# Compressed branch's product on 128 rows, gates kept as 1 / gate, negated scale behind the rope

## The chip, the cores and the metric

The kernel runs on one core of one Trainium2 chip. Times are device microseconds (us) of that core; the time of a kernel is the median of its runs. The engines are TensorE (PE; its weight loads are listed as PEld), VectorE (DVE), ScalarE (ACT), GpSimd (POOL) and SyncE (SP, which issues most DMAs).

## What is computed

A decoder trunk of four layers over 256 tokens of 1024 features. Each layer is a token mixer and a squared-ReLU MLP, both with an RMS norm ahead and a residual sum. The change lies in the first layer's mixer, an attention with three branches per head: keys and values compressed over blocks of 32 tokens at stride 16 (15 blocks), selected blocks (here with 256 tokens all blocks that are not in the future), and a window. Each branch has its own softmax, and a sigmoid gate per token and head weighs its output. Cut to that:

```python
def _nsa_mixer(h, w_in, q_gain, k_gain, cmp_pos, w_cmp, w_out, cos, sin):
    q, kc, vc, ks, vs, kw, vw, gates = jnp.split(h @ w_in, ...)
    q = _apply_rope(_rms_norm(q, q_gain), cos, sin)          # 8 heads of 128
    kc, ks, kw = [_apply_rope(_rms_norm(k, k_gain[i]), cos, sin) for i, k in ...]
    gates = jax.nn.sigmoid(gates)
    kc = jnp.einsum('bnlgd,lde->bnge', kc[:, cidx] + cmp_pos[0], w_cmp[0])
    vc = jnp.einsum('bnlgd,lde->bnge', vc[:, cidx] + cmp_pos[1], w_cmp[1])
    ...
    p_c = _masked_softmax(q kc * scale, cmp_end <= t)
    o_c = jnp.einsum('bqghn,bngd->bqghd', p_c, vc)
    ... # p_s, o_s of the selected blocks; p_w, o_w of the window
    o = g[:, :, 0] * o_c + g[:, :, 1] * o_s + g[:, :, 2] * o_w
    return o @ w_out
```

## The kernel before

Everything is float32, and products with weights are made of three float32r products: each weight is split into a rounded part wh (ACT, L159) and the rest wl (DVE, L160), and L184 to L186 multiply them with the two parts of the input. Tokens lie in two tiles t of 128.

The function `nsa` projects in six chunks (`chunk`, 384 or 512 columns; 280 with the gates), into queries, keys and values. Chunks 0 to 3 give all keys, the first group's values, the gates and the queries of heads 0 to 3; `compress` makes the compressed keys (in `kcat`) and values `vcmp`, 32 rows of which two groups of 15 are used. Then come attention passes (`attend`) over units of a head h and a token tile t. The first pass has the eight units of heads 0 to 3; chunks 4 and 5 bring the second group's values and the queries of heads 4 to 7; the second pass has the eight units of these. The output products (`Out`, L212 to L214, "acc" in the trace) follow.

For a unit, `scores` adds masks and products of queries and keys in PSUM (t = 0: L579 to L583, t = 1: L594 to L604), takes maxima (DVE, L585, L606, L609), multiplies them with `nrq`, the negated scale of the query (L611), and ACT makes the exponentials of the three branches with their sums (L615). From the sums DVE makes the branches' weights in three steps, L618 (a maximum with 1e-30), L619 (the reciprocal) and L620 (times the gate), and scales the exponentials with them (L622, L623). `mix` then transposes the scaled exponentials on PE (L633 for two branches, L637 for the 32 compressed columns), ACT copies them to SBUF (PT, L635, and PTc, L639), and PE adds up the three branches in one accumulator `po`: two or four products with 128 rows (L642) and, last, one with 32 rows (L643). Each of these products is two instructions in the trace. ACT and DVE split the result (L89, L90).

`queries` computes the scale `rq` of each query with a power on POOL (in `head_scale`, L385), then `nrq` on DVE (L471), then the rope on DVE (L392, L393, L402), and queues the transposes (L459).

The order of the instructions on each engine is set by the scheduler of the layer under the kernel; it takes them from the order in which the code stands and from what it reckons to be ready. Each engine runs its own queue in order. In the passes the scheduler puts projection products (L184 to L186) and output products between the units' work on PE. Here the gates' lines before:

```python
gt = wp.tile([P, 24], F32, tag="gt", name="gt")
nc.scalar.activation(gt, o[:, 256:280], AF.Exp, scale=nrx[t])
nc.vector.tensor_scalar(gt, gt, 1.0, None, op0=ALU.add)
nc.vector.reciprocal(gates[:, t].rearrange("p a b -> p (a b)"), gt)
```

Of the kernel before, what the change touches and what calls it, by code (L numbers as in the profile page):

```python
# [10 lines left out]
F32 = mybir.dt.float32  # L11
F32R = mybir.dt.float32r
AF = mybir.ActivationFunctionType
ALU = mybir.AluOpType
AX = mybir.AxisListType

P = 128
# [6 lines left out]
DH = 128  # L24
# [43 lines left out]
def trunk(ctx: ExitStack, tc: tile.TileContext, A: dict, out: bass.AP):  # L68
    nc = tc.nc
# [354 lines left out]
    def nsa(n, first):  # L424
        aT = n.xT
        nxt = start_norm(4)
        with tc.tile_pool(name="nsa", bufs=1) as sp:
# [9 lines left out]
            gates = sp.tile([P, NT, NH, 3], F32, name="gates")  # L437
            rq = sp.tile([P, NT, NH], F32, name="rq")
            nrq = sp.tile([P, NT, NH], F32, name="nrq")
            vcmp = sp.tile([32, DH], F32, name="vcmp")  # L440
            quarters = sp.tile([P, 32], F32, name="quarters")
            oT = act.tile([P, KT, 2, NT, P], F32R, tag="aT", name="oT")
            with tc.tile_pool(name="nsw", bufs=2) as wp:
# [24 lines left out]
                def queries(t, src, h0, nh):  # L468
                    v = src.rearrange("p (h d) -> p h d", d=DH)
                    head_scale(wp, v, nh, he[t], rq[:, t, h0:h0 + nh])  # L470
                    nc.vector.tensor_scalar(nrq[:, t, h0:h0 + nh], rq[:, t, h0:h0 + nh], -1.0, None, op0=ALU.mult)  # L471
                    r = rope(wp, src, nh, G[:, t, 0, 0:1].to_broadcast([P, nh, DH]),
                             G[:, t, 1, 0:1].to_broadcast([P, nh, DH]))
                    transpose_to([(qT[:, h0:h0 + nh, t * P:(t + 1) * P], (0, nh))], [r[:, h] for h in range(nh)])


# [7 lines left out]
                def chunk(ci):  # L484
                    width = (offs[ci + 1] - offs[ci]) // 8
                    if ci == 0:
                        views = col_chunk(A["nsa_w"], 0, width, first)
                        ahead.extend(col_chunk(A["nsa_w"], offs[1], width, None, (0,)))
                        gain_tables(nc.vector, G, A["rope"], A["nsa_gain"], A["nsa_gsw"], 4)
                    elif ci == 1:  # L490
                        views = ahead + col_chunk(A["nsa_w"], offs[1], width, None, (1,))
                    else:
                        views = col_chunk(A["nsa_w"], offs[ci], width)
                    os_ = proj(aT, views, width, "AC")
                    for t in range(NT):
                        o = os_[t]
                        ts_ = slice(t * P, (t + 1) * P)
                        if not he:
                            stats()
                        if ci == 0:  # L500
                            kn = normed(wp, o[:, :256], 2, he[t])
                            r = rope(wp, kn, 2, G[:, t, 0, 1:2].to_broadcast([P, 2, DH]),
                                     G[:, t, 1, 1:2].to_broadcast([P, 2, DH]))
                            vc = wp.tile([P, 2, DH], F32, tag="vc", name="vc")
                            nc.scalar.mul(vc, o[:, 256:].rearrange("p (a b) -> p a b", b=P), rx[t])
                            cols = [kcT[:, kv, :, 1 + 16 * t:17 + 16 * t].rearrange("p r (n g) -> p g n r", g=2)
                                    for kv in range(2)]
                            transpose_to([(cols[0], (0, 2)), (cols[1], (2, 4))],
                                         [r[:, 0], r[:, 1], vc[:, 0], vc[:, 1]])
                        elif ci == 1:  # L510
                            kn = normed(wp, o, 4, he[t])
                            g1, g2 = ([G[:, t, i, 2 + k:3 + k].to_broadcast([P, 2, DH]) for k in range(2)]
                                      for i in range(2))
                            r = rope(wp, kn, 4, g1, g2, True)
                            base = 288 * t
                            transpose_to([(kcat[:, :, base:base + P], (0, 2)),
                                          (kcat[:, :, base + P:base + 2 * P], (2, 4))], [r[:, h] for h in range(4)])
                        elif ci == 2:
                            queries(t, o, 0, 4)
                        elif ci == 5:  # L520
                            queries(t, o[:, :384], 5, 3)
                        else:
                            g = ci - 3
                            nc.scalar.mul(vv[:, t, :, g], o[:, :256].rearrange("p (a b) -> p a b", b=P), rx[t])
                            if ci == 3:
                                gt = wp.tile([P, 24], F32, tag="gt", name="gt")
                                nc.scalar.activation(gt, o[:, 256:280], AF.Exp, scale=nrx[t])
                                nc.vector.tensor_scalar(gt, gt, 1.0, None, op0=ALU.add)
                                nc.vector.reciprocal(gates[:, t].rearrange("p a b -> p (a b)"), gt)
                            else:  # L530
                                queries(t, o[:, 256:384], 4, 1)

                def tables():
                    nc.sync.dma_start(mks, A["nsa_mask"])
                    nc.vector.tensor_copy(mk, mks)
                    nc.gpsimd.tensor_copy(identr, ident)
                    nc.sync.dma_start(posT, A["nsa_pos"])
                    nc.sync.dma_start(quarters, A["cmp_sum"])
                    nc.gpsimd.memset(kcT[:, :, :, 34:36], 0.0)
                    nc.gpsimd.tensor_copy(kcT[:, :, :, 0:34:33], posT.rearrange("p k (a r) -> p k r a", a=2))  # L540

                def compress(kv):
# [17 lines left out]
                    pt = bank("B", "pt")  # L560
                    if kv == 0:
                        nc.tensor.matmul(pt[:, :32], lhsT=part, rhs=quarters, start=True, stop=True)
                        for g in range(2):
                            nc.scalar.copy(kcat[:, g, 256:288], pt[:, :32])
                    else:
                        nc.tensor.matmul(pt[:32, :DH], lhsT=quarters, rhs=part, start=True, stop=True)
                        nc.scalar.copy(vcmp, pt[:32, :DH])

                def scores(h, t):

# [44 lines left out]
                        nc.scalar.activation(pr[:, a:b], views[br], AF.Exp, bias=nm[:, br:br + 1], scale=r_,  # L615
                                             accum_out=sums[:, br:br + 1])
                    co = sm.tile([P, 3], F32, tag="co", name="co")
                    nc.vector.tensor_scalar(co, sums, 1e-30, None, op0=ALU.max)  # L618
                    nc.vector.reciprocal(co, co)  # L619
                    nc.vector.tensor_mul(co, co, gates[:, t, h])  # L620
                    v = pr[:, :2 * w].rearrange("p (a b) -> p a b", a=2)
                    nc.vector.tensor_tensor(v, v, co[:, 0:2, None].to_broadcast([P, 2, w]), op=ALU.mult)  # L622
                    nc.vector.tensor_scalar(pr[:, 2 * w:2 * w + 32], pr[:, 2 * w:2 * w + 32], co[:, 2:3], None,  # L623
# [3 lines left out]
                def mix(h, t, pr):  # L627
# [7 lines left out]
                    nc.scalar.copy(PT[:, :2 * nb], pp[:, :2 * w].rearrange("p (a b) -> p a b", b=P))  # L635
                    po = bank("C", "po")
                    nc.tensor.transpose(po[:32, :P], pr[:, 2 * w:2 * w + 32], ident)  # L637
                    PTc = wp.tile([32, P], F32, tag="PTc", bufs=3, name="PTc")
                    nc.scalar.copy(PTc, po[:32, :P])  # L639
                    ov = po[:, P:256]  # L640
                    for k in range(2 * nb):
                        nc.tensor.matmul(ov, lhsT=vv[:, k % nb, k // nb, g], rhs=PT[:, k], start=k == 0, stop=False)  # L642
# [554 lines left out]
```

## Time and profile before

| | us |
|---|---|
| median of 3 runs | 1197.43 (1195.81 to 1198.53) |
| profiled execution | 1196.0 |
| its span, first to last instruction | 1194.2 |
| PE busy | 1174.7 (98% of the span) |
| DVE busy | 780.2 (65%) |
| ACT busy | 623.5 (52%) |
| POOL busy | 35.0 (3%) |

The span is that of the traced instructions; the execution's own time has 1.8 us around it. Matmuls are pipelined and their ends are modelled, so a PE that is shown busy need not be at its peak: how fast it goes is read from the distance between the starts of its instructions. A wait is put down to what the instruction waited for last.

### The profile page before, as it was taken

How to read it: one execution, taken by the hardware profiler on the slowest of the kernel's cores; microseconds unless marked ns; L12 is line 12 of the kernel's file. 1: busy time of each engine (PE TensorE's matmuls, PEld its weight loads, DVE VectorE, ACT ScalarE, POOL GpSimd, SP SyncE). 2: the span in 40 equal slices, each digit the busy share in tenths (PEclk: the TensorE clock that was granted, in tenths of full speed). 3: DMA queues.
4: the chain of work that ended last, by engine and by line, in shares of the span. 5: the costliest groups of instructions: out<-in, count | busy, mean ns of one | idle time of the engine just before them, and what ended most of it. 6: DMA issues, size and time to landing. Idle time of an engine off the chain costs nothing.

```text
span 1194.2 us, 17643 instructions
## 1 busy us (share of the span) xinstructions
PE 1174.7 (98%) x7042; PEld 1010.6 (85%) x7042; DVE 780.2 (65%) x1203; ACT 623.5 (52%) x1027; POOL 35.0 (3%) x47
## 2 busy tenths in 40 slices
PE   7999999999999999999999999999999999999998
PEld 5888988888888898888889898888888789888886
DVE  7678686566585577565566578556558876666553
ACT  6477554444465555444454276444447665544441
POOL 1200000000000000000001100000001010000000
PEclk9999999999999999999999999999999999999999
DMA  8553154554554425554546736355454633555440
GB/s 310 189 184 142 70 213 152 201 212 158 195 176 163 167 85 207 212 211 147 206 147 194 247 142 246 142 212 210 144 201 159 224 114 110 208 201 190 173 176 36
DMA packets 35074, 211.24 MB, mean 177 GB/s; under 512 B 4528, under 2 KB 7472, under 8 KB 11440
## 3 DMA queue, kind: packets, MB, share of 16 engines
q1 hardware_dynamic: 30672, 199.94, 46.7%
q0 software_dynamic: 1424, 5.75, 1.8%
q10 hardware_dynamic: 2896, 4.42, 1.1%
q8 instruction: 55, 0.90, 0.3%
q14 instruction: 27, 0.22, 0.1%
HBM read 207.87 MB, written 2.23 MB: 176 GB/s over the span
## 4 chain that ended last, share of the span: by engine, by line
PE 64%; issue 26%; DVE 5%; DMA 1%; POOL 1%; ACT 1%; SPq 0%; ACTq 0%; POOLq 0%; DVEq 0%
PE projT L205 22%; PE dn L184 7%; PE dn L186 7%; PE dn L185 7%; PE ab L873 2%; DVE wl L160 2%; PE acc L212 2%; PE acc L213 2%; PE acc L214 2%; PE proj L184 2%; PE proj L186 2%; PE proj L185 2%; PE po L642 1%; POOL rs L385 1%; ACT wh L159 1%
## 5 line engine op out<-in xcount | busy, mean ns | idle before, releaser
L160 DVE TENSOR_TENSOR wl<-raw,wh 128x1024 fp32r<-128x1024 f32 (+2 forms) x376 | 445.9, 1211 | 188.8 <-ACT wh L159 184.1
L159 ACT CAST wh<-raw 128x1024 fp32r<-128x1024 f32 (+2 forms) x376 | 379.7, 1040 | 208.6 <-PE dn L186 111.2
L205 PE MATMUL projT<-xT,wh 128*128 128x512 f32 x1152 | 361.6, 396 | 0.3 <-DVE xT L101 0.3
L205 PEld LDWEIGHTS projT<-xT,wl 128*128 128x128 f32 x1152 | 215.3, 188 | 49.7
L205 PE MATMUL projT<-xT,wl 128*128 128x256 f32 x1152 | 225.9, 278 | 0.0
L184 PE MATMUL dn<-wh,u 128*128 128x512 f32 x512 | 202.7, 396 | 0.0
L186 PE MATMUL dn<-wh,u 128*128 128x512 f32 x512 | 202.0, 395 | 0.0
L185 PE MATMUL dn<-wl,u 128*128 128x512 f32 x512 | 201.4, 393 | 0.0
L205 PEld LDWEIGHTS projT<-xT,wh 128*128 128x128 f32 x1152 | 178.3, 189 | 3.5 <-DVE xT L101 0.5
L186 PEld LDWEIGHTS dn<-wh,u 128*128 128x128 f32 x512 | 96.4, 188 | 22.3
L185 PEld LDWEIGHTS dn<-wl,u 128*128 128x128 f32 x512 | 96.4, 188 | 20.8
L184 PEld LDWEIGHTS dn<-wh,u 128*128 128x128 f32 x512 | 96.5, 188 | 20.3
L184 PE MATMUL proj<-wh,xT 128*128 128x512 f32 (+2 forms) x224 | 87.2, 391 | 8.0 <-ACT wh L159 7.6
L310 ACT COPY b<-projT 128x256 f32<-128x256 f32 x128 | 41.2, 374 | 93.9 <-PE projT L205 93.6
L185 PE MATMUL proj<-wl,xT 128*128 128x512 f32 (+2 forms) x224 | 85.9, 383 | 0.0
L186 PE MATMUL proj<-wh,xT 128*128 128x512 f32 (+2 forms) x224 | 85.8, 384 | 0.0
L311 DVE TENSOR_TENSOR s<-projT,b 128x256 f32<-128x256 f32 x128 | 48.1, 418 | 55.0 <-ACT b L310 55.0
L89 ACT CAST u<-q 128x1024 fp32r<-128x1024 f32 x32 | 33.6, 1049 | 82.7 <-DVE q L313 82.6
L212 PE MATMUL acc<-oT,wh 128*128 128x256 f32 x256 | 73.6, 292 | 0.1
L213 PE MATMUL acc<-oT,wh 128*128 128x256 f32 x256 | 72.9, 286 | 0.0
L214 PE MATMUL acc<-oT,wl 128*128 128x256 f32 x256 | 71.0, 284 | 0.0
L90 DVE TENSOR_TENSOR u<-q,u 128x1024 fp32r<-128x1024 f32 x32 | 39.2, 1226 | 34.6 <-ACT u L89 34.6
(252 smaller groups left out, 1243.8 us busy)
## 6 DMA issues: line engine op xcount, KB each, us to landing
raw<-in_down SPq DMA_DIRECT2D x64, 1024.0 KB, 4.9
raw<-in_up SPq DMA_DIRECT2D x63, 1024.0 KB, 4.8
raw<-in_sb_w SPq DMA_DIRECT2D x12, 1024.0 KB, 4.8
raw<-in_moba_w SPq DMA_DIRECT2D x12, 1024.0 KB, 4.9
raw<-in_conv_w SPq DMA_DIRECT2D x8, 1024.0 KB, 4.9
st<-dr POOLq DMA_DIRECT2D x16, 287.0 KB, 4.7
raw<-in_nsa_w SPq DMA_DIRECT2D x4, 1024.0 KB, 6.3
rawc<-in_nsa_cmp SPq DMA_DIRECT2D x4, 1024.0 KB, 4.8
```

The lines of the kernel that those rows point to most:

```text
L90: return a, nc.vector.tensor_sub(lo, src, hi.bitcast(F32))
L159: nc.scalar.copy(wh[:, :w], r)
L160: nc.vector.tensor_sub(wl[:, :w], r, wh[:, :w].bitcast(F32))
L184: nc.tensor.matmul(o, lhsT=aT[:, kt, 0, t, :], rhs=wh, start=first, stop=False)
L185: nc.tensor.matmul(o, lhsT=aT[:, kt, 0, t, :], rhs=wl, start=False, stop=False)
L186: nc.tensor.matmul(o, lhsT=aT[:, kt, 1, t, :], rhs=wh, start=False, stop=last)
L205: nc.tensor.matmul(o[:, :width], lhsT=v[kt][part][:, f * P:(f + 1) * P], rhs=rhs, start=kt == 0 and part == 0, stop=kt == KT - 1 and part ...
L212: nc.tensor.matmul(o, lhsT=wh, rhs=aT[:, kt, 0], start=first, stop=False, skip_group_check=True)
L213: nc.tensor.matmul(o, lhsT=wh, rhs=aT[:, kt, 1], start=False, stop=False, skip_group_check=True)
L214: nc.tensor.matmul(o, lhsT=wl, rhs=aT[:, kt, 0], start=False, stop=last, skip_group_check=True)
L310: nc.scalar.copy(b, o[:, S:])
L311: nc.vector.tensor_add(s[:, f], o[:, :S], b)
```

## The change

The compressed branch's last product is made on 128 rows instead of 32. `vcmp` and three tiles `wcmp`, which take the place of PTc's three buffers in turn, have 128 rows, are set to zero once on POOL (in `tables`), and only their first 32 rows are written later. The gates are kept as 1 + exp(-x), that is 1 / gate: their reciprocal falls away, and in `scores` one instruction makes max(sums, 1e-30) times that, with the reciprocal behind it. In `queries`, the line with `nrq` stands behind the rope.

```diff
@@ -437,7 +437,9 @@
             gates = sp.tile([P, NT, NH, 3], F32, name="gates")
             rq = sp.tile([P, NT, NH], F32, name="rq")
             nrq = sp.tile([P, NT, NH], F32, name="nrq")
-            vcmp = sp.tile([32, DH], F32, name="vcmp")
+
+            vcmp = sp.tile([P, DH], F32, name="vcmp")
+            wcmp = [sp.tile([P, P], F32, name=f"wcmp{i}") for i in range(3)]
             quarters = sp.tile([P, 32], F32, name="quarters")
             oT = act.tile([P, KT, 2, NT, P], F32R, tag="aT", name="oT")
             with tc.tile_pool(name="nsw", bufs=2) as wp:
@@ -468,9 +470,9 @@
                 def queries(t, src, h0, nh):
                     v = src.rearrange("p (h d) -> p h d", d=DH)
                     head_scale(wp, v, nh, he[t], rq[:, t, h0:h0 + nh])
-                    nc.vector.tensor_scalar(nrq[:, t, h0:h0 + nh], rq[:, t, h0:h0 + nh], -1.0, None, op0=ALU.mult)
                     r = rope(wp, src, nh, G[:, t, 0, 0:1].to_broadcast([P, nh, DH]),
                              G[:, t, 1, 0:1].to_broadcast([P, nh, DH]))
+                    nc.vector.tensor_scalar(nrq[:, t, h0:h0 + nh], rq[:, t, h0:h0 + nh], -1.0, None, op0=ALU.mult)
                     transpose_to([(qT[:, h0:h0 + nh, t * P:(t + 1) * P], (0, nh))], [r[:, h] for h in range(nh)])
 
 
@@ -523,10 +525,10 @@
                             g = ci - 3
                             nc.scalar.mul(vv[:, t, :, g], o[:, :256].rearrange("p (a b) -> p a b", b=P), rx[t])
                             if ci == 3:
-                                gt = wp.tile([P, 24], F32, tag="gt", name="gt")
+
+                                gt = gates[:, t].rearrange("p a b -> p (a b)")
                                 nc.scalar.activation(gt, o[:, 256:280], AF.Exp, scale=nrx[t])
                                 nc.vector.tensor_scalar(gt, gt, 1.0, None, op0=ALU.add)
-                                nc.vector.reciprocal(gates[:, t].rearrange("p a b -> p (a b)"), gt)
                             else:
                                 queries(t, o[:, 256:384], 4, 1)
 
@@ -537,6 +539,8 @@
                     nc.sync.dma_start(posT, A["nsa_pos"])
                     nc.sync.dma_start(quarters, A["cmp_sum"])
                     nc.gpsimd.memset(kcT[:, :, :, 34:36], 0.0)
+                    for z in [vcmp] + wcmp:
+                        nc.gpsimd.memset(z, 0.0)
                     nc.gpsimd.tensor_copy(kcT[:, :, :, 0:34:33], posT.rearrange("p k (a r) -> p k r a", a=2))
 
                 def compress(kv):
@@ -564,7 +568,7 @@
                             nc.scalar.copy(kcat[:, g, 256:288], pt[:, :32])
                     else:
                         nc.tensor.matmul(pt[:32, :DH], lhsT=quarters, rhs=part, start=True, stop=True)
-                        nc.scalar.copy(vcmp, pt[:32, :DH])
+                        nc.scalar.copy(vcmp[:32], pt[:32, :DH])
 
                 def scores(h, t):
 
@@ -615,9 +619,8 @@
                         nc.scalar.activation(pr[:, a:b], views[br], AF.Exp, bias=nm[:, br:br + 1], scale=r_,
                                              accum_out=sums[:, br:br + 1])
                     co = sm.tile([P, 3], F32, tag="co", name="co")
-                    nc.vector.tensor_scalar(co, sums, 1e-30, None, op0=ALU.max)
+                    nc.vector.scalar_tensor_tensor(co, sums, 1e-30, gates[:, t, h], op0=ALU.max, op1=ALU.mult)
                     nc.vector.reciprocal(co, co)
-                    nc.vector.tensor_mul(co, co, gates[:, t, h])
                     v = pr[:, :2 * w].rearrange("p (a b) -> p a b", a=2)
                     nc.vector.tensor_tensor(v, v, co[:, 0:2, None].to_broadcast([P, 2, w]), op=ALU.mult)
                     nc.vector.tensor_scalar(pr[:, 2 * w:2 * w + 32], pr[:, 2 * w:2 * w + 32], co[:, 2:3], None,
@@ -635,8 +638,9 @@
                     nc.scalar.copy(PT[:, :2 * nb], pp[:, :2 * w].rearrange("p (a b) -> p a b", b=P))
                     po = bank("C", "po")
                     nc.tensor.transpose(po[:32, :P], pr[:, 2 * w:2 * w + 32], ident)
-                    PTc = wp.tile([32, P], F32, tag="PTc", bufs=3, name="PTc")
-                    nc.scalar.copy(PTc, po[:32, :P])
+                    PTc = wcmp[0]
+                    wcmp.append(wcmp.pop(0))
+                    nc.scalar.copy(PTc[:32], po[:32, :P])
                     ov = po[:, P:256]
                     for k in range(2 * nb):
                         nc.tensor.matmul(ov, lhsT=vv[:, k % nb, k // nb, g], rhs=PT[:, k], start=k == 0, stop=False)
```

The scheduler makes another order out of this, in the first layer's attention only. SP's order is unchanged. Three places follow, with the buffers' numbers behind the names.

PE in the first pass, between the second and the third mix, to the end of the third, before (proj is a projection product, po the mix's accumulator, pr the scaled exponentials):

```order
L186 MATMUL proj_1017<-wh_999,xT_83 128x384
L184 MATMUL proj_1017<-wh_1003,xT_83 128x384
L594 MATMUL sc1_857<-mk_93,identr_85 128x128
L604 MATMUL sc1_857<-kcat_96,qT_95 128x256
L637 MATMUL po_802<-ident_76,pr_752 32x128
L185 MATMUL proj_1017<-wl_1004,xT_83 128x384
L186 MATMUL proj_1017<-wh_1003,xT_83 128x384
L184 MATMUL proj_1017<-wh_1003,xT_83 128x384
L185 MATMUL proj_1017<-wl_1004,xT_83 128x384
L594 MATMUL sc0_894<-mk_93,identr_85 128x128
L642 MATMUL po_802<-PT_800,vv_97 128x128 x2
L643 MATMUL po_802<-PTc_804,vcmp_101 128x128
```

The same stretch of PE in the new order, from the end of the second mix:

```order
L647 MATMUL po_767<-wcmp1_103,vcmp_101 128x128
L603 MATMUL sc0_845<-kcat_96,qT_95 128x32
L608 MATMUL sc0_845<-kcat_96,qT_95 128x256
L184 MATMUL proj_1004<-wh_986,xT_83 128x384
L636 MATMUL pp_794<-ident_76,pr_752 128x128 x2
L598 MATMUL sc1_851<-mk_93,identr_85 128x128
L640 MATMUL po_799<-ident_76,pr_752 32x128
L608 MATMUL sc1_851<-kcat_96,qT_95 128x256
L185 MATMUL proj_1004<-wl_987,xT_83 128x384
L646 MATMUL po_799<-PT_797,vv_97 128x128 x2
L647 MATMUL po_799<-wcmp2_104,vcmp_101 128x128
```

Of the projection products between the second and the third mix there are two in the new order, six before; from the first to the eighth mix there are 28 and were 38, and the rest stands behind the eighth.

DVE at the queries of heads 5 to 7, second token tile, before (m1 and m2 are the rope's products, ss and rq the scale's):

```order
L384 TENSOR_SCALAR ss_1180<-ss_1180,heps_251 128x3
L392 TENSOR_TENSOR m1_1185<-proj_1114,G_91 128x384
L471 TENSOR_SCALAR nrq_100<-rq_99 128x3
L393 TENSOR_TENSOR m2_1186<-proj_1114,G_91 128x384
L585 TENSOR_REDUCE mx_1190<-sc_1191 128x2
L402 TENSOR_TENSOR m1_1185<-m1_1185,m2_1186 128x384
```

And now:

```order
L384 TENSOR_SCALAR ss_1167<-ss_1167,heps_254 128x3
L392 TENSOR_TENSOR m1_1171<-proj_1101,G_91 128x384
L393 TENSOR_TENSOR m2_1172<-proj_1101,G_91 128x384
L475 TENSOR_SCALAR nrq_100<-rq_99 128x3
L589 TENSOR_REDUCE mx_1177<-sc_1178 128x2
L402 TENSOR_TENSOR m1_1171<-m1_1171,m2_1172 128x384
```

L471, now L475, has moved behind the rope's second product. At the first token tile of the same heads it stood behind both products already.

PE in front of the transposes of these queries' first token tile, now (acc is an output product):

```order
L603 MATMUL sc0_1200<-kcat_96,qT_95 128x32
L608 MATMUL sc0_1200<-kcat_96,qT_95 128x256
L608 MATMUL sc1_1206<-kcat_96,qT_95 128x256
L212 MATMUL acc0_1522<-oT_106,wh_1484 128x256
L213 MATMUL acc0_1522<-oT_106,wh_1484 128x256
L214 MATMUL acc0_1522<-oT_106,wl_1485 128x256
L212 MATMUL acc0_1522<-oT_106,wh_1484 128x256
L213 MATMUL acc0_1522<-oT_106,wh_1484 128x256
L461 MATMUL pt_1236<-ident_76,m1_1159 128x128 x3
```

Five output products stand between the scores and the transposes; with those ahead of the scores there were 14 from the end of the projection on before.

## Rows read from the trace of the kernel before

**Rows 1.** The page: span, and PE's busy time (share) xinstructions.
```profile
span 1194.2 us, 17643 instructions
PE 1174.7 (98%) x7042; PEld 1010.6 (85%) x7042; DVE 780.2 (65%) x1203; ACT 623.5 (52%) x1027; POOL 35.0 (3%) x47
```

**Rows 2.** Windows: stretch, length, busy PE PEld DVE ACT POOL, clock, DMA.
```profile
60.50:89.40 28.90, 28.90 (x185) 24.74 (x185) 22.99 (x85) 23.32 (x77) 0.55 (x1) 1.00 0.54 186
...
107.00:133.00 26.00, 25.71 (x170) 21.23 (x169) 16.75 (x73) 18.80 (x73) 0.00 (x0) 1.00 0.12 42
133.00:240.00 107.00, 107.00 (x606) 93.07 (x606) 72.64 (x92) 56.92 (x80) 0.00 (x0) 1.00 0.50 179
```

**Rows 3.** Waits of PE: who for whom, total us, times, longest.
```profile
PE pt L566 <- ACT part L559: 0.7, 1, 0.7
...
PE pt L459 <- DVE ss L384: 0.3, 1, 0.3
...
PE pt L459 <- DVE mx L609: 0.2, 1, 0.2
```

**Rows 4.** Timeline, a mix in the first pass: start, us, engine, line, operation.
```profile
77.16 0.34 PE L185 MATMUL proj<-wl,xT 128*128 128x384 f32 x1
77.33 1.06 PE L642 MATMUL po<-PT,vv 128*128 128x128 f32 x8
78.32 0.48 PE L643 MATMUL po<-PTc,vcmp 32*128 32x128 f32 x2
78.73 0.44 PE L186 MATMUL proj<-wh,xT 128*128 128x384 f32 x1
...
77.23 0.97 PEld L642 LDWEIGHTS po<-PT,vv 128*128 128x128 f32 x8
78.32 0.29 PEld L643 LDWEIGHTS po<-PTc,vcmp 32*128 32x128 f32 x2
78.73 0.19 PEld L186 LDWEIGHTS proj<-wh,xT 128*128 128x128 f32 x1
```

**Rows 5.** By source line: count, ns min/median/max, first and last start.
```profile
L642 PE MATMUL po<-PT,vv x96: 272/275/377, 63.1 to 132.0; 128*128 128x128 f32 x96
L643 PE MATMUL po<-PTc,vcmp x32: 270/321/372, 63.6 to 132.4; 32*128 32x128 f32 x32
```

**Rows 6.** Timeline of PE in the second pass, ahead of a mix.
```profile
114.59 0.47 PE L212 MATMUL acc<-oT,wh 128*128 128x256 f32 x1
115.17 1.16 PE L642 MATMUL po<-PT,vv 128*128 128x128 f32 x8
```

**Rows 7.** Timeline of DVE, first unit: the small instructions.
```profile
58.24 0.23 DVE L611 TENSOR_SCALAR nm<-mx,nrq 128x3 f32<-128x3 f32 x1
...
60.38 0.16 DVE L620 TENSOR_TENSOR co<-co,gates 128x3 f32<-128x3 f32 x1
60.57 0.42 DVE L622 TENSOR_TENSOR pr<-pr,co 128x256 f32<-128x256 f32 x1
```

**Rows 8.** Timeline between the passes; in brackets idle time and releaser.
```profile
105.08 0.17 DVE L471 TENSOR_SCALAR nrq<-rq 128x3 f32<-128x3 f32 x1 [0.51 <-POOL rq L385]
...
106.02 0.28 PE L213 MATMUL acc<-oT,wh 128*128 128x256 f32 x1
106.14 0.28 PE L214 MATMUL acc<-oT,wl 128*128 128x256 f32 x1
106.65 0.52 PE L459 MATMUL pt<-ident,m 128*128 128x128 f32 x3 [0.23 <-DVE mx L609]
```

**Rows 9.** Timeline of POOL at the start of the run.
```profile
0.73 0.16 POOL L539 MEMSET kcT<- 128x64 f32 x1 [0.29 <-POOLq L1186]
6.66 0.46 POOL L536 CAST identr<-ident 128x128 fp32r<-128x128 f32 x1 [5.77 <-DMA ident<-in_ident]
```

**Rows 10.** Timeline of DVE behind the gates, ahead of the first unit.
```profile
57.68 0.42 DVE L585 TENSOR_REDUCE mx<-sc 128x2 f32<-128x256 f32 x1 [1.73 <-PE sc L583]
```

**Rows 11.** Windows with ACT alone, first pass without its end.
```profile
60.50:83.00 22.50, 21.09 (x71) 1.00 0.54 187
```

## Prediction

> **What bounds the kernel now.** I read the page's head first: TensorE (PE) has records for 1174.7 of 1194.2 us [rows 1]. A busy PE need not be a PE at its peak, so I then read the stage that the change touches by stretches. The two attention passes of the first layer lie at about 60.5 to 89.4 and 107 to 133 us; PE is busy 28.90 of 28.90 and 25.71 of 26.00 there, at its full granted clock, and in the 107 us behind them all the time [rows 2]. The list of PE's waits in the whole run has three of note there: 0.7 us just before the first pass, and 0.3 and 0.2 in front of the queries' transposes between the passes [rows 3]. So PE sets the pace, and time that one of its instructions takes in the passes is time of the kernel; time saved on DVE counts only where PE waits for DVE. Behind 133 us PE has no gap that could swallow a gain, so what is saved stays saved.
>
> **The product on 128 rows.** One such product (L643) ends the mix of each of 16 units (head, token tile), as two instructions each, 32 in all [rows 5]. In front of it stand products with 128 rows, L642. Eight of them last 1.06 us and one 275 ns, so seven steps take 0.785 and one step 0.112 us [rows 4, 5]. The last of the eight thus starts at 77.33 + 7 x 0.112 = 78.115, but L643 only at 78.32: 0.205 instead of 0.112. Its two instructions then last from 78.32 to 78.73, 0.41 us, where two L642 would take 0.224 [rows 4]. Together 0.615 instead of 0.336: 0.28 us. The rows show what happens: the weights of L643, with 32 active rows, are loaded at 78.32, the moment its matmul begins, and those of the next product with 128 rows at 78.73, so neither load runs under the product before it; L642's loads, from 77.23 on, run ahead of their products [rows 4]. With vcmp and the other operand at 128 rows the product has the form of L642. Bounds for its two instructions with the entry: 0.336 (L642's step) and 0.615 (as now). I take the first, since form, type and accumulator are those of L642. 16 x 0.28 = **4.5 us less**, all on PE.
>
> The Trainium skill has a rule on either side. "TensorE: Matmul & The Clock Gate", section "Step-by-step: what each phase is for", says that the time of a weight load goes with the columns and that the row count does not matter; by that the padding would save nothing and this term would be 0. "TensorEngine Tiling (Array Packing)", section "Key Properties", says that a change of tiling mode drains TensorE; by that the term stands at 4.5. The loads at 78.32 and 78.73 agree with the second.
>
> **What the padding adds.** Four memsets of 128x128 on POOL. The nearest row is 0.16 us for 128x64 [rows 9]; so 0.16 to 0.32 each (the fixed part alone, or twice the elements), 0.6 to 1.3 together. They stand behind that memset at 0.73 us, and POOL then idles 5.77 us until the identity has landed at 6.66 [rows 9]: hidden. Without that cover they would delay the cast of the identity, which PE wants only in the first pass (L579), by at most 1.3 us. No DMA is added or moved, and SP's queue is unchanged. The copies of the transposed weights (L639) still write 32 rows.
>
> **One DVE step less in the weights' scale.** The maximum, the reciprocal and the product with the gate (L618 to L620) become two instructions. L620 starts 0.19 us ahead of L622 [rows 7]: that step goes. The new first instruction, with two operations, isn't in the trace; the nearest rows with three elements last 0.16 (L620, one operation) and 0.23 us (L611, two) [rows 7], I take the second. So the chain from exponentials to transposes gets 0.12 to 0.19 us shorter a unit. It counts only where PE waits for that chain. In the second pass some such waits are hidden under the modelled ends, the largest at 115.17, where L642 starts 0.58 us after an output product whose step is 0.12 [rows 6, 8]. I count 0.3 us for all of these (0 to 1.2, eight units with 0.15 each). The two reciprocals of the gates vanish in front of 1.73 us of DVE's idleness: nothing [rows 10].
>
> **The negated scale behind the rope.** DVE stands still for POOL's power at each L471, 0.51 us at 105.08, with the rope's L393 and L402 queued behind it, and PE's transposes behind those wait 0.23 us until 106.65 [rows 8]. In the new order only the second tile's L471 passes L393, so that its rope ends up to 0.5 us earlier: the 0.23 goes. The first tile's order there is as before, so the 0.28 of its transposes stays [rows 3]. At the queries of heads 0 to 3 the same move helps DVE too, but the list of waits has none of PE for those [rows 3]: nothing. The Exp of the gates now writes where the add reads: nothing.
>
> **What the new order gives back.** Counted in the two orders, 38 projection products stand between the first and the eighth mix before, 28 now; ten, of 0.17 us each (77.16 to 77.33 [rows 4]), moved behind. PE's work in the first pass falls from 28.9 to 28.9 - 8 x 0.28 - 1.7 = 25.0 us, and ACT, with the same work, is busy 23.3 of it [rows 2]. PE remains the longer by 1.7, but each mix now reaches ACT's copies sooner: 0.4 us given back (0 to 1.6). In front of the first tile's transposes between the passes stand 5 output products instead of 14, so 9 x 0.12 = 1.1 us of PE work [rows 8] no longer covers DVE's rope. But ten projection products more stand between the last mix and that point, in which DVE gets its weight splits (L160) done. I take 0.1 given back (-0.5 to 1.1). By the last mix 61 output products are done, 60 before: no work has left the passes.
>
> **The sum.** -4.5 - 0.3 - 0.2 + 0.4 + 0.1 = -4.5 us. The profiled execution took 1196.0 us (span 1194.2 and 1.8 around it): 1191.5. The median of the three runs, 1197.4, stands 1.4 above it, so I forecast **1192.9 us**. A measurement of this kernel tells about 0.2% from no change, 2.4 us.
>
> **The rivals.**
> - *ACT takes over.* For: ACT was busy 21.09 of 22.50 us up to 83 us [rows 11], and fillers have gone from between the mixes. If ACT keeps those 1.4 us of idleness, does its other 2.2 us (23.32 - 21.09) unhindered, and the last mix (1.4 us, 77.33 to 78.73 [rows 4]) follows behind, the first pass ends after 21.1 + 1.4 + 2.2 + 1.4 = 26.1 instead of 25.0. That is 0.7 beyond the 0.4 counted; and if in the second pass, whose ACT is busy 18.80 of 26 [rows 2], each of eight units waits 0.2 more, 1.6 besides. Gain 2.2: 1195.2 us. Against: part of ACT's idleness was itself waiting for PE.
> - *The waits go too.* Shorter chain at its bound (1.2), sooner rope, between the passes the lower bound (0.5 less), nothing given back in the first: 4.5 + 1.2 + 0.2 + 0.5 = 6.4: 1191.0 us.
> - *The padding saves nothing*, the rows' count not mattering and the pause belonging to the end of an accumulation. Then only the other terms remain, about zero together: 1197.4 us. Against: the pause stands in front of L643 as well.
> - *Slower.* PE takes its instructions in order, and each mix waits for ACT's copies, which are queued behind exponentials of later units. In the second pass the first four mixes have no output product between them in the new order; before there was one. If each of the 16 mixes waited as the one at 115.17 (0.46 over its step) [rows 6], that would cost 7.4 and give 1192.9 + 7.4 = 1200.3 us. It decides from 0.28 us a mix on. Against: only one wait of that size is in the trace.
>
> **How the numbers follow.** Forecast (1191.5 to 1194.5): 0.55. ACT takes over: 0.18, half of it beyond 2.4 us of gain. Waits go too: 0.09. Padding saves nothing: 0.06. Slower: 0.12. Faster 0.55 + 0.09 + 0.09 = 0.73, same 0.09 + 0.06 = 0.15, slower 0.12. The range goes from 1190.7, below the second rival, to 1197.2, which takes in the first and leaves out most of the last two, some 0.17 in all.
>
> **What would show it.** Right: the product's instructions start 0.11 us apart with loads ahead of them, the eighth mix ends near 85 us and the last near 128, and everything behind lies some 4.5 us earlier. Wrong: a step of 0.2 stays; or PE stands in front of the mixes, released by ACT's copies; or the gap in front of the queries' transposes grows past 0.5 us.

## The result

The changed kernel takes 1190.05 us (median of 5 runs, 1189.1 to 1193.81); the kernel before, timed beside it, takes 1198.06 (5 runs, 1195.81 to 1198.99). The ratio is 0.994, with a 95% interval from 0.9921 to 0.996: faster by 0.4 to 0.8%. Timed once more, beside the experiments, the same code gave 1191.04 us against 1196.65, ratio 0.995 [0.9936, 0.9964]. The forecast was 1192.9 in a range from 1190.7 to 1197.2. The sign is right; the first median lies 0.65 us below the range, the second inside it, so the gain was sized too small. How much, and in which step, is read from the trace.

### The profile after

The head of the page, which answers [rows 1] (span; busy time of each engine, its share and instructions):

```profile
span 1187.3 us, 17631 instructions
PE 1168.0 (98%) x7042; PEld 1008.6 (85%) x7042; DVE 777.2 (65%) x1185; ACT 622.0 (52%) x1027; POOL 33.0 (3%) x51
```

PE has as many instructions as before and 6.7 us less of busy time; the span is 6.9 us shorter, and the profiled execution took 1189.1 instead of 1196.0. DVE has lost 18 instructions, 16 of the units and two of the gates, and POOL has won the four memsets. PE still sets the pace in both passes and behind them; the windows that answer [rows 2] (stretch, length, busy PE PEld DVE ACT POOL, clock, DMA):

```profile
60.00:84.40 24.40, 24.40 (x175) 22.09 (x175) 21.62 (x76) 22.15 (x76) 0.55 (x1) 1.00 0.58 192
102.00:125.90 23.90, 23.90 (x183) 21.75 (x182) 15.99 (x66) 17.78 (x73) 0.00 (x0) 1.00 0.14 45
125.90:233.00 107.10, 107.10 (x606) 93.08 (x605) 72.59 (x92) 57.02 (x81) 0.00 (x0) 1.00 0.50 179
```

Behind the last mix the same 606 instructions of PE fill the same 107 us as before, now about 7 us earlier: nothing was lost again there. PE's granted clock is 1.00 in these windows in both traces, the upper of its two levels (2.4 GHz).

A mix with as many products as the one of [rows 4] (there the fifth, here the sixth), in the trace after: PE, then its weight loads.

```profile
77.33 1.16 PE L646 MATMUL po<-PT,vv 128*128 128x128 f32 x8
78.33 0.39 PE L647 MATMUL po<-wcmp,vcmp 128*128 128x128 f32 x2
78.55 0.60 PE L636 MATMUL pp<-ident,pr 128*128 128x128 f32 x4
...
77.33 0.97 PEld L646 LDWEIGHTS po<-PT,vv 128*128 128x128 f32 x8 [0.19 <-ACT wcmp L643]
78.22 0.30 PEld L647 LDWEIGHTS po<-wcmp,vcmp 128*128 128x128 f32 x2
78.44 0.47 PEld L636 LDWEIGHTS pp<-ident,pr 128*128 128x128 f32 x4
```

The two instructions of the product begin at 78.33, and what follows at 78.55: 0.22 us, where it was 0.41. Their loads begin at 78.22, 0.11 ahead of the product, under the products before it, and the next loads at 78.44, ahead of 78.55. Before, each of these two loads began when its matmul did [rows 4].

The 0.41 us hold one more slow step. The second instruction of that product before (its load, its matmul) and, below, the second one of the mix of [rows 6]:

```profile
78.43 0.18 PEld L643 LDWEIGHTS po<-PTc,vcmp 32*128 32x128 f32 x1
78.53 0.27 PE L643 MATMUL po<-PTc,vcmp 32*128 32x128 f32 x1
...
115.38 0.39 PE L642 MATMUL po<-PT,vv 128*128 128x128 f32 x2
```

The first one began at 78.32, so there are 0.21 us between two instructions of one form, although the second load runs 0.10 ahead of its matmul. The mix that had waited until 115.17 [rows 6] takes the same 0.21 to its second instruction, at 128 rows. So PE stops ahead of the product with 32 rows and behind it, and the slow step inside is the one that is also seen behind a wait.

To compare kernels, the trace is cut at four places that every one of them has: the first mix (start of its 32- or 128-row product), the end of the eighth, the start of the ninth's product, and the end of the sixteenth (an end is the start of PE's next instruction). Worked out from the timelines of PE, in us, with the number of projection products in the first stretch and output products in the last:

| | first pass | between | second pass | sum | projection, output |
|---|---|---|---|---|---|
| before | 25.40 | 23.31 | 20.30 | 69.0 | 38, 15 |
| after | 21.13 | 23.26 | 18.18 | 62.6 | 28, 26 |

The sum falls by 6.4 us. Of the 6.9 us of the span the other half microsecond lies ahead of the first mix (63.59 us in one trace, 63.00 in the other). That place moves between 62.35 and 63.81 us over the ten traces of this study, in which it doesn't follow the edits: the unchanged kernel after gave 62.38 when profiled again. What lies behind the last mix, 1057.1 to 1060.1 us to the start of PE's last instruction, doesn't follow them either; a wait of the later convolution for DMA alone takes 1.0 us in the kernel with the padding alone and 3.2 us in the kernel after, profiled again. So the sums of the table are what the edits are compared by, beside the times.

### The profile page after: what moved, and what is told of

The parts are those of the page before. It is cut to its first block, busy times and chain, and to the rows that moved or that the text cites. A ratio compares the mean times of both kernels' runs of the same rounds, so it can differ in the third digit from the quotient of the medians.

```text
span 1187.3 us, 17631 instructions
## 1 busy us (share of the span) xinstructions
PE 1168.0 (98%) x7042; PEld 1008.6 (85%) x7042; DVE 777.2 (65%) x1185; ACT 622.0 (52%) x1027; POOL 33.0 (3%) x51
## 4 chain that ended last, share of the span: by engine, by line
PE 63%; issue 27%; DVE 5%; DMA 2%; ACT 1%; POOL 1%; SPq 0%; ACTq 0%; DVEq 0%; POOLq 0%
PE projT L205 23%; PE dn L184 7%; PE dn L186 7%; PE dn L185 7%; PE ab L877 2%; PE acc L212 2%; PE acc L213 2%; DVE wl L160 2%; PE acc L214 2%; PE proj L186 1%; PE proj L184 1%; PE proj L185 1%; PE po L646 1%; POOL rs L385 1%; ACT wh L159 1%
```

## The experiments

My theory is the prediction's: the 32 rows stop PE twice in each mix, and the padding is nearly all of the gain. Its rivals are that the rows don't matter and something else in the change shortens the passes, and that the waits (or the new order of work) carry a good part.

### Each part alone

Only the padding; PE's and ACT's orders are then those of before, row for row:

```diff
-            vcmp = sp.tile([32, DH], F32, name="vcmp")
+            vcmp = sp.tile([P, DH], F32, name="vcmp")
+            wcmp = [sp.tile([P, P], F32, name=f"wcmp{i}") for i in range(3)]
...
+                    for z in [vcmp] + wcmp:
+                        nc.gpsimd.memset(z, 0.0)
...
-                        nc.scalar.copy(vcmp, pt[:32, :DH])
+                        nc.scalar.copy(vcmp[:32], pt[:32, :DH])
...
-                    PTc = wp.tile([32, P], F32, tag="PTc", bufs=3, name="PTc")
-                    nc.scalar.copy(PTc, po[:32, :P])
+                    PTc = wcmp[0]
+                    wcmp.append(wcmp.pop(0))
+                    nc.scalar.copy(PTc[:32], po[:32, :P])
```

> Only the padding (vcmp and three wcmp tiles of 128 rows, zeroed once); gates and negated scale as before. The orders of PE, ACT and DVE are those of the kernel before, row for row. Theory 'rows': each of the 16 products starts 0.11 instead of 0.21 us after the one in front, and its instructions are 0.11 instead of 0.21 us apart, 0.28 to 0.30 us a mix; PE has nothing to wait for, so 4.0 to 4.8 us less in all. Rival 'order': PE arrives sooner at copies that ACT hasn't made, most is given back as waits in front of the mixes, and the gain stays under 2.5 us.

Only the gates; PE and ACT then have the order of the kernel after:

```diff
-                                gt = wp.tile([P, 24], F32, tag="gt", name="gt")
+                                gt = gates[:, t].rearrange("p a b -> p (a b)")
...
-                                nc.vector.reciprocal(gates[:, t].rearrange("p a b -> p (a b)"), gt)
...
-                    nc.vector.tensor_scalar(co, sums, 1e-30, None, op0=ALU.max)
+                    nc.vector.scalar_tensor_tensor(co, sums, 1e-30, gates[:, t, h], op0=ALU.max, op1=ALU.mult)
                     nc.vector.reciprocal(co, co)
-                    nc.vector.tensor_mul(co, co, gates[:, t, h])
```

> Only the gates kept as 1 / gate, with one instruction of DVE less a unit; product on 32 rows, negated scale ahead of the rope. PE, ACT and POOL have the orders of the changed kernel, so this one edit makes the new order. Theory 'rows': 1.0 to 2.2 us faster than before, from waits between and in the passes; the product's steps stay at 0.21. Rival 'order': 4 us or more.

Only the line with `nrq` behind the rope; PE and ACT have the order of before:

```diff
-                    nc.vector.tensor_scalar(nrq[:, t, h0:h0 + nh], rq[:, t, h0:h0 + nh], -1.0, None, op0=ALU.mult)
                     r = rope(...)
+                    nc.vector.tensor_scalar(nrq[:, t, h0:h0 + nh], rq[:, t, h0:h0 + nh], -1.0, None, op0=ALU.mult)
```

> Only the negated scale behind the rope; PE, ACT and POOL have the orders of the kernel before. Both theories: the second tile's rope between the passes ends some 0.45 us sooner, PE's 0.23 us in front of its transposes go, 0 to 0.5 us faster in all, too little to tell by the times; the timeline between the passes shows it.

And the whole change with the product's operands cut to their first 32 rows again, everything else as in after:

```diff
-                        nc.tensor.matmul(ov, lhsT=vcmp, rhs=PTc, start=False, stop=True)
+                        nc.tensor.matmul(ov, lhsT=vcmp[:32], rhs=PTc[:32], start=False, stop=True)
```

> The changed kernel with its four zeroed tiles, but the product reads only their first 32 rows. The orders of all engines are those of the changed kernel. Theory 'rows': the steps of 0.21 us come back, and the kernel is 4.3 to 4.8 us slower than the changed one, so 1.5 to 2.5 us faster than before. Rival 'order': the kernel keeps 4 us or more of the gain, because the new order and the shorter chain brought it.

What was measured; the ratio is to the kernel before, at 1196.97 us (28 runs):

| kernel | us (runs) | ratio, 95% | first pass | between | second pass | sum |
|---|---|---|---|---|---|---|
| only the padding | 1193.25 (7) | 0.9968 [0.9956, 0.9981] | 22.91 | 23.24 | 18.06 | 64.2 |
| only the gates | 1195.95 (11) | 0.9991 [0.9982, 0.9999] | 23.53 | 23.78 | 20.32 | 67.6 |
| only `nrq` | 1196.62 (11) | 0.9997 [0.9988, 1.0005] | 25.43 | 22.92 | 20.29 | 68.6 |
| after, 32 rows read | 1194.95 (9) | 0.9979 [0.9969, 0.999] | 23.54 | 23.37 | 20.31 | 67.2 |

The three parts are worth 4.78, 1.37 and 0.36 us by their sums, 6.51 together; the whole change is worth 6.43. So they add up, and nothing that one part gains is eaten by another. The times say the same with less sharpness: the padding alone is faster, the gates alone are just distinguishable from no change, `nrq` alone is not. By the sums all four came out inside what was expected of them; by the times the padding alone gains 3.7 us, under the 4.0 expected, with an interval of 2.3 to 5.3. Taking the padding out of the whole change costs 67.2 - 62.6 = 4.65 us by the sums.

**The padding.** With it alone the tenth mix reads (PE, second pass of that kernel):

```profile
111.91 0.47 PE L212 MATMUL acc<-oT,wh 128*128 128x256 f32 x1
112.49 1.16 PE L646 MATMUL po<-PT,vv 128*128 128x128 f32 x8
113.48 0.39 PE L647 MATMUL po<-wcmp,vcmp 128*128 128x128 f32 x2
113.70 0.38 PE L636 MATMUL pp<-ident,pr 128*128 128x128 f32 x2
```

and with the whole change but 32 rows read, in the first pass:

```profile
76.87 0.48 PE L647 MATMUL po<-wcmp,vcmp 32*128 32x128 f32 x2
77.29 0.66 PE L636 MATMUL pp<-ident,pr 128*128 128x128 f32 x4
...
76.87 0.29 PEld L647 LDWEIGHTS po<-wcmp,vcmp 32*128 32x128 f32 x2
77.28 0.42 PEld L636 LDWEIGHTS pp<-ident,pr 128*128 128x128 f32 x4
```

The one reads 0.22 us (113.48 to 113.70), the other 0.42, with both loads starting when their matmul does. PE's order with the padding alone is that of before, and with 32 rows read it is that of the kernel after, so the rows alone make the difference. Over the 16 mixes the entries into the product sum to 3.28 us with 32 rows and 1.79 with 128, the product itself to 6.62 and 3.00 (3.33 in the whole change). These steps save 5.1 us (4.8 in the whole change), more than the 4.78 (4.65) by which the stretches fall: 0.3 us (0.1) come back as longer steps elsewhere in the passes. The gap in front of this mix, 112.49 - 111.91 less a step of 0.12 for the output product, is still there with the padding alone: what is not the rows, it leaves.

**The gates.** They move nothing on DVE that PE is seen to wait for in the list of waits; what they change is the order. In the first pass ten projection products of 0.174 us fewer, 1.74 us, and the pass is 1.87 shorter. Between the passes stand these ten more and ten output products of 0.12 fewer (35, not 45), and two products of masks have come there from the second pass (0.15 and 0.08 us): 0.8 us more work, and the stretch is 0.47 longer. In the second pass are 11 output products more, 1.3 us, and the two products of masks fewer, and it is as long as before, 20.32 for 20.30. So most of the gain of this part, 1.4 us, arises in the second pass, where about 1.1 us of additional work costs nothing; some 0.3 arise between the passes and 0.1 in the first. The tenth mix of this kernel, PE and the copy by ACT that it needs last:

```profile
113.97 1.05 PE L640 MATMUL po<-PT,vv 128*128 128x128 f32 x8
114.96 0.48 PE L641 MATMUL po<-PTc,vcmp 32*128 32x128 f32 x2
115.37 0.28 PE L635 MATMUL po<-ident,pr 128*32 128x128 f32 x1
115.41 0.31 PE L593 MATMUL sc<-mk,identr 128*128 128x128 f32 x1
...
113.07 0.25 ACT L637 COPY PTc<-po 32x128 f32<-32x128 f32 x1
```

I took every start in the second pass that lies over 0.12 us behind the usual step of its pair of instructions (the median over the ten traces): before, four of them with 1.14 us together, the largest the one of [rows 6], and none of them in the list of waits; with the padding alone 1.19, with the gates alone and in the kernel after none. The sums depend on which step is called usual (with the shortest instead, 1.2 to 1.4 before and 0 to 0.5 with the gates alone). These gaps are where the output products went.

What closed the largest of them is the order. In the trace of before (DVE, PE, ACT):

```profile
112.86 0.23 DVE L623 TENSOR_SCALAR pr<-pr,co 128x32 f32<-128x32 f32 x1
...
113.69 0.60 PE L633 MATMUL pp<-ident,pr 128*128 128x128 f32 x4
...
114.38 0.59 ACT L635 COPY PT<-pp 128x512 f32<-128x512 f32 x1 [0.41 <-PE pp L633]
114.86 0.25 ACT L639 COPY PTc<-po 32x128 f32<-32x128 f32 x1
```

DVE has scaled the exponentials at 113.09, and PE takes up their transposes only at 113.69, behind score products. ACT waits 0.41 us for them; its second copy ends at 115.11, and the mix begins at 115.17 [rows 6]. The gap is a round trip from PE over ACT back to PE, with too little other work for PE in it. In all 16 units of the kernel before, PE's transposes begin 0.27 to 3.19 us after DVE's scaling (L622) has ended, so PE had no wait for that chain which 0.2 us less in it could have ended. With the gates alone the same copy ends at 113.32 and the mix begins 0.65 us later, because transposes and scores of the next unit stand in between. Of the smaller gaps, those before 127.94 and 128.57 also end within 0.06 us of the end of an ACT instruction (a split of the result and a copy); the one before 122.91 stays open. The old chain in the new order wasn't run, so what the shorter chain does beyond changing the order isn't shown.

**The negated scale.** DVE, between the passes of the kernel with `nrq` alone, second tile:

```profile
104.77 0.55 DVE L393 TENSOR_TENSOR m<-proj,G 128x384 f32<-128x384 f32 x1
105.36 0.17 DVE L473 TENSOR_SCALAR nrq<-rq 128x3 f32<-128x3 f32 x1
```

The scale stands behind the rope's L393 and no longer waits 0.51 us for POOL [rows 8]; the stretch between the passes is 0.39 shorter.

### How many rows stop PE

Theory: the pause belongs to products on part of the array's rows. By how many rows, the change can't tell. The whole change, with the first 64 and the first 96 rows read, one run of each beside the kernel before at 1196.65 us and the kernel after, unchanged:

```diff
-                        nc.tensor.matmul(ov, lhsT=vcmp, rhs=PTc, start=False, stop=True)
+                        nc.tensor.matmul(ov, lhsT=vcmp[:64], rhs=PTc[:64], start=False, stop=True)
```

> The changed kernel, its product reading the first 64 rows of the zeroed tiles; the orders of all engines are those of the changed kernel. Theory 'any smaller row form stops PE': the steps of 0.21 us are back in full, 0.41 us for the two instructions, and the passes from the first to the last mix take about 67.2 us as with 32 rows. Rival 'it goes with the rows left out': about half, 0.3 us for the two and 65 us for the passes.

```diff
-                        nc.tensor.matmul(ov, lhsT=vcmp, rhs=PTc, start=False, stop=True)
+                        nc.tensor.matmul(ov, lhsT=vcmp[:96], rhs=PTc[:96], start=False, stop=True)
```

> The same with 96 rows. Theory 'form': 96 rows need the whole array like 128, so 0.22 us for the two instructions and 62.6 us from the first to the last mix, as in the changed kernel. Rival 'every count but 128 stops PE': 0.41 and about 67.2.

The kernel after, unchanged:

> The changed kernel once more, beside the others on the same chip: 0.992 to 0.996 of the time before, 62.6 us from the first to the last mix.

With 64 rows (PE, first pass):

```profile
79.55 1.16 PE L646 MATMUL po<-PT,vv 128*128 128x128 f32 x8
80.64 0.48 PE L647 MATMUL po<-wcmp,vcmp 64*128 64x128 f32 x2
81.06 0.66 PE L636 MATMUL pp<-ident,pr 128*128 128x128 f32 x4
```

With 96 rows, the same mix:

```profile
77.80 1.16 PE L646 MATMUL po<-PT,vv 128*128 128x128 f32 x8
78.80 0.39 PE L647 MATMUL po<-wcmp,vcmp 96*128 96x128 f32 x2
79.02 0.60 PE L636 MATMUL pp<-ident,pr 128*128 128x128 f32 x4
```

64 rows take 0.42 us, as 32 do, and the stretch is 67.25 us (1194.79 us in all; with 32 rows 67.2). 96 rows take 0.22, as 128 do, and the stretch is 62.6 (1190.11 us); the kernel after, profiled again, has 62.55 (1191.04 us, 5 runs). So the cost doesn't grow or fall with the rows: two forms stop PE fully, two not at all.

This bears on the two rules that the prediction set side by side. The Trainium skill, "TensorEngine Tiling (Array Packing)", section "Key Properties", has a change of tiling mode drain TensorE, and its section "Available Configurations" lists forms of 32, 64 and 128 rows, none of 96. The 0.42 us at 32 and 64 rows and the 0.22 at 96 agree with both. That list also has a form of 128 rows and 32 columns; the transposes that the traces show as 128*32 cause no stop (115.37 and 115.41 above), so not every such form costs one here. The Trainium skill, "TensorE: Matmul & The Clock Gate", section "Step-by-step: what each phase is for", says of the weight load's own time that the row count doesn't matter, and this nearly holds: 182 ns with 32 rows, 192 with 128. That the padding would save nothing didn't follow from it: what the rows change is when a load can begin.

### The scale on POOL

After the change the first tile's transposes still waited for DVE, whose `nrq` waits 0.51 us for POOL. In the kernel after, on DVE and PE between the passes:

```profile
98.51 0.17 DVE L475 TENSOR_SCALAR nrq<-rq 128x3 f32<-128x3 f32 x1 [0.51 <-POOL rq L385]
...
99.33 0.28 PE L213 MATMUL acc<-oT,wh 128*128 128x256 f32 x1
99.75 0.52 PE L461 MATMUL pt<-ident,m 128*128 128x128 f32 x3
```

The transposes start 0.42 us after an output product whose step is 0.12: 0.3 us lost. POOL can negate its own result:

```diff
-                    nc.vector.tensor_scalar(nrq[:, t, h0:h0 + nh], rq[:, t, h0:h0 + nh], -1.0, None, op0=ALU.mult)
+                    nc.gpsimd.tensor_scalar(nrq[:, t, h0:h0 + nh], rq[:, t, h0:h0 + nh], -1.0, None, op0=ALU.mult)
```

> The changed kernel with the negated scale made on POOL, right behind the power, so that no instruction of DVE waits for POOL at the queries. Some output products move a few places on PE. Expected: the first tile's transposes between the passes lose the 0.3 us that PE still waits for DVE, the passes take 62.0 to 62.6 us, 0 to 0.6 us faster than the changed kernel. Rival: POOL's small instructions take 0.2 to 0.5 us each and the maxima times nrq wait for them; no gain or 0.5 us lost.

POOL, DVE and PE at the same place:

```profile
97.00 0.89 POOL L385 TENSOR_TENSOR rq<-ss,nhalf 128x3 f32<-128x3 f32 x1 [3.18 <-DVE ss L384]
97.98 0.53 POOL L475 TENSOR_SCALAR nrq<-rq 128x3 f32<-128x3 f32 x1
...
97.40 0.55 DVE L383 TENSOR_REDUCE ss<-sq 128x3 f32<-128x384 f32 x1
97.87 0.55 DVE L402 TENSOR_TENSOR m<-m,m 128x384 f32<-128x384 f32 x1
...
98.69 0.28 PE L213 MATMUL acc<-oT,wh 128*128 128x256 f32 x1
98.81 0.49 PE L461 MATMUL pt<-ident,m 128*128 128x128 f32 x3
```

DVE goes from the second tile's sums straight to the rope's L402, and the transposes follow the output product by 0.12 us. The stretch between the passes falls from 23.26 to 22.80 us, the sum from 62.6 to 62.0. The time is 1188.98 us (5 runs, 1188.28 to 1189.61), ratio 0.9936 [0.9924, 0.9949] to before. It lies below both medians of the kernel after; of the 2 us to the one beside it (1191.04) the sums account for 0.55, of which 0.12 is one output product that now stands behind the last mix. The intervals overlap, so the rest isn't claimed.

## Why the prediction was right in sign and short in size

- **What bounds.** Right. PE is busy throughout both passes after the change too, and the 107 us behind them hold the same work in the same time: all that was saved in the passes stayed saved.
- **The product on 128 rows, 4.5 us.** Right, in mechanism and nearly in size: 4.78 us with the padding alone, 4.65 when taken out of the whole. An entry fell from 0.205 to 0.112 us, and the two instructions from 0.41 to 0.22 or less, the lower bound that was chosen. That 16 x 0.28 came so close is in part luck: these steps save 0.32 us a mix (0.30 in the whole change), and a little comes back elsewhere. *The padding saves nothing* is refuted.
- **The memsets.** Right. They take 0.20 us for `vcmp` and 0.49 for the three others, inside the 0.6 to 1.3 of the prediction, and POOL then idles 5.19 us before the cast of the identity (POOL at the start, kernel after):

```profile
0.82 0.20 POOL L543 MEMSET vcmp<- 128x128 f32 x1
0.96 0.49 POOL L543 MEMSET wcmp<- 128x128 f32 x3
6.64 0.45 POOL L538 CAST identr<-ident 128x128 fp32r<-128x128 f32 x1 [5.19 <-DMA ident<-in_ident]
```

- **One DVE step less, 0.3 us.** This term and the next failed, in the mechanism. The chain itself became shorter by 0.2 us, the upper end of the 0.12 to 0.19 that was counted: the new instruction lasts 0.16 us, the lower of the two rows (all 16 of them; ns min, median, max, first and last start, form):

```profile
L622 DVE SCALAR_TENSOR_TENSOR co<-sums,gates x16: 148/161/164, 59.4 to 118.1; 128x3 f32<-128x3 f32 x16
```

  But the term counts the gap at 115.17 [rows 6] as a wait of PE for this chain, and the trace of before has it end with ACT's copies of transposes that PE itself took up 0.6 us after DVE was done. The step that failed is this reading of the gaps, and with it the price of the order: the edit put 11 output products into the second pass, into gaps of 1.1 us together, and all went. The prediction counted the work that the order moves (61 output products by the last mix, which is what the trace shows) and priced it only as a loss.
- **What the new order gives back, 0.4 and 0.1 us.** Wrong: nothing. With the gates alone the first pass is 1.87 us shorter with 1.74 us of products fewer in it, and between the passes 0.47 longer with 0.8 more, so that it gains 0.1 and 0.3 there besides the 1.1 of the second pass. ACT, whose copies this term feared, is busy 22.15 of the 24.40 us from 60 to 84.4, PE all of them; *ACT takes over* is refuted, and so is *slower*, whose gaps in front of the mixes closed instead of spreading.
- **The scale behind the rope, 0.2 us.** Right, and slightly more: 0.36 alone, 0.41 in the new order (67.63 of the gates alone less 67.22 of the change with 32 rows). The first tile's wait of about 0.3 stayed, as foretold, until the scale went to POOL. One new wait came that no term had, of scores on a copy of the queries by ACT (0.25 us at 97.66 in the kernel after); it is there with the padding alone too (0.2 us), and inside the stretch between the passes, which didn't become longer.
- **The sum.** Against -4.5 stand -4.8 for the padding, -1.4 for the gates and their order (foretold: -0.3 + 0.4 + 0.1 = +0.2) and -0.4 for the scale: some 2 us more, of which 1.6 is the order. That is the total of the rival *the waits go too*, 6.4 us of gain and 1191.0, which had a chance of 0.09. That the totals agree is in part luck: the rival's 1.2 us of a shorter chain are about what the second pass gained, but from the order, and its 0.5 between the passes came out as 0.3. Its time lies between the two medians of the kernel after (1190.05 and 1191.04).
- **The landmarks.** "The eighth mix ends near 85": 84.13. "The last near 128": 125.57, earlier because of the second pass; 0.6 us of both lie ahead of the first mix, in the part that moves from run to run. "Some 4.5 us earlier" behind: about 7.

## What to carry to other kernels

In a chain of small products, look at where the weight loads start: if the load of one product begins only when its matmul does, and the next one's too, that product's form is stopping TensorE, and zeros in the unused rows cost less than the stop (0.3 us a product here). If an edit changes the order, price the moved work at the place where it arrives too: filler that lands in gaps of the bounding engine is free there, and the gaps may be ones that no list of waits shows, only the distance of starts. Before a gap is put down to a chain, follow it back to the instruction that ended it: here it was a round trip over ACT, and DVE had long been done. Parts that looked like nothing (0.36 us of a scale's wait, 1.4 us of an order) were worth over a third of the padding together, and in the times they could hardly be told from no change, only in the trace's stretches.

## What was not expected of the hardware

- Products on 64 rows stop TensorE exactly as those on 32 do (0.42 us for two instructions with the entry at 0.2), and those on 96 rows not at all (0.22 us). The weights' load itself takes about the same time in all of them; by source line, from the kernels with 64 and with 96 rows (ns min, median, max):

```profile
L647 PEld LDWEIGHTS po<-wcmp,vcmp x32: 182/184/186, 63.7 to 130.6; 64*128 64x128 f32 x32
```

```profile
L647 PEld LDWEIGHTS po<-wcmp,vcmp x32: 190/191/192, 63.4 to 125.9; 96*128 96x128 f32 x32
```

  184 against 191 ns: it is when the load may begin, not how long it lasts, that costs.
- A transpose whose weights have 128 rows but 32 columns doesn't stop TensorE: in the kernel with the gates alone the one at 115.37 is followed by the next product at 115.41, 0.04 us later.
- An instruction on three elements a partition, multiplied by a constant, took 0.53 us on POOL behind its power (0.24 behind the second tile's), and 0.17 on DVE, where it had cost 0.51 us of waiting besides. The longer instruction on the idle engine was the cheaper one.
